# The start of a pooling-mixer layer: ScalarE and VectorE in source order through the first two products

## The chip, the cores and the metric

The kernel runs on one core of a Trainium2 chip. The core has TensorE (matmuls, into eight PSUM banks), VectorE, ScalarE and GpSimd (elementwise work), and SyncE, which here only issues DMAs; DMAs are also issued from ScalarE's and GpSimd's queues. An engine executes its own instructions in the order in which they stand in the program, and waits on semaphores for what others make. The time is device microseconds of one execution, of which several are run and the median is given. One execution is also taken by the hardware profiler, and every row of a profile below is from it.

## The reference

One layer over x (1 x 4096 x 1024, float32):

```python
normed = rms_norm(h, norm_w)
u, gate = split(normed @ in_w, 2)              # in_w 1024 x 2048
pooled = trailing means of u (windows 2, 4, 8, 16; one per group of 256 columns) - u
mixed = einsum('bsgc,gcd->bsgd', pooled, group_w) + group_b
h = h + (mixed * scale * silu(gate)) @ out_w   # out_w 1024 x 1024
out = rms_norm(h, final_norm_w)
```

## The kernel before

**Products.** Every large product (gate half, u half, output) is made with a seven-product scheme for 2 x 2 blocks (P1 to P7): 28 products for the gate half ("a", four blocks of 1024 rows), 28 for the u half ("b"), 56 for the output ("o"). Float32 operands are split in a high and a low part, and each product is three matmuls, high by high, high by low, low by high. One product of "a" or "b" is 48 matmul groups of 128x512 on TensorE. The group's linear map commutes with the trailing mean, so it is folded into the columns of in_w once, at the start ("fold", L406, with its evictions L424 and L171).

**The tiles.** `w[P1]`, `w[P2]` ... hold the split weights of a product, two tiles each (one for each half of its depth). `op0` to `op3` (op_85 to op_88 in the order listings) hold split activations, two for a product. Banks 0 to 7 are bank_69 to bank_76 in these listings. `st` and `vt` tiles are general 128x1024 buffers, taken and given back in turn; `early` tiles are room inside weight tiles that no product uses yet. `ru[q, k]` are quarters of in_w to be folded, loaded by `load_wut`.

**Row scales.** Rows of x are loaded (`load_row`), squared and summed on ScalarE (`square_row`), and `stats` makes 1/sqrt: square root on ScalarE, reciprocal on VectorE (L218), then four small operations that sharpen it (the first block's on VectorE, L157 and L224; later blocks' on GpSimd, L230 to L235). For block 0, `split_rs` and `spread_rs` broadcast the scales over the partitions through TensorE (L472) and bank 7. For later blocks the scales are stored to DRAM (L455) and loaded back as a broadcast (L492), both issued by GpSimd. `normalize` multiplies x with them, and `split_halves` makes an operand's high part (copy on ScalarE) and low part (subtraction on VectorE).

**Sums for the later products.** S1 to S4 are differences and sums of blocks of x, T1 to T4 of weights. `form_s4` makes S4, P3's operand; `rest_of_first` makes P5's weights (T1 of the scheme), P4's (T4) and the copies for P3 during the first block.

**What sets the order.** A scheduler orders instructions by priority and by when their inputs are ready. Inside stretches where `in_line[0]` is True, each instruction that `lined()` records is put behind the one made before it on that engine, so that ScalarE and VectorE keep source order. Before the change this stretch ends ahead of the first product; behind it single edges (`tc.issue_after`) and `tc.high_priority()` hold parts of the order. `run(n, between, behind)` writes product n, calls `between[g]` ahead of its g-th group (key 8: behind the last), and `behind` names the group that is put after the broadcast.

**After P1 and P2.** From L1321 on, a loop runs over the remaining products: it loads, forms and splits operands some products ahead, and evicts and pools behind. Block 1 of the gate half follows block 0's P3. Its P1 and P2 add up in banks 0 to 3; P7 comes third and needs these banks emptied.

Of the kernel before, what the change touches and what calls it, by code (L numbers as in the profile page):

```python
# [61 lines left out]
def kernel(  # L62
# [208 lines left out]
    def pair(cs, h, kh):  # L271
        k = 4 * kh + 2 * h
        return cs[k : k + 2]
# [105 lines left out]
    def load_wut(q, k, queues=(nc.sync,)):  # L379
        r = take("p (k t c) -> p k t c", early5, k=2, t=4)  # L380
        by = 2 // len(queues)
        for n, queue in enumerate(queues):
            kk = slice(n * by, (n + 1) * by)
            queue.dma_start(out=r[:, kk], in_=wut[q, k // 2, :, kk])
        return r
# [12 lines left out]
    def fold(g, r, ps2, halves=(0, 1)):  # L398

        pairs = [(r, g)] if not isinstance(r, list) else [(r[0], g[0]), (r[0], g[1]), (r[1], g[0])]  # L400
        for kk in halves:
            for j in range(2):
                for t in range(2):
                    for m, (a, b) in enumerate(pairs):
                        maps = b[:, 2 * j + t, :]
                        latest[0] = nc.tensor.matmul(  # L406
                            ps2[kk][:, j * 256 : (j + 1) * 256],
                            a[:, kk, 2 * j + t, :],
                            maps if len(pairs) == 1 else woven(maps),
                            start=t + m == 0,  # L410
                            stop=t == 1 and m == len(pairs) - 1,
                        ).ins
        if len(pairs) == 1 and 1 in halves:
            give(r)
# [593 lines left out]
    def load(n):  # L1008
        kind, b, i = step(n)
        if kind == "o":  # L1010
            load_o(b, i)
        elif kind:
            load_in(kind == "b", b, i)
# [82 lines left out]
    for j in range(2, 4):  # L1096
        load_row(0, 0, j)
# [6 lines left out]
    ru[1, 4] = load_wut(1, 4)  # L1104
# [6 lines left out]
    v1[0] = take()  # L1111
# [24 lines left out]
    square_row(0, 0, 3)  # L1136
    for j in range(4):
        load_row(0, 1, j, early if j < 3 else None)
    load(1)
# [7 lines left out]
    fold(gw[1], ru[1, 4], pairs_of[1], (0,))  # L1147
    wut_high(1, 2, w[P2][0])
    spread_rs(0)
    fold(gw[1], ru[1, 4], pairs_of[1], (1,))  # L1150
# [3 lines left out]
    for kk in range(2):  # L1154
        evict_fold(o[1], 4, kk, pairs_of[1], False)
    form(0)
    split_step(0)
    first_split = latest_split[0]
    split_scaled(w[P1][0], g0[0], pair(norm_c, 0, 0))
# [9 lines left out]
    in_line[0] = False  # L1169
    stores.extend((wvd[n], o[j]) for j, n in enumerate((0, 2, 1, 3)))  # L1170

    def second_side(h):

        if h == 1:
            with tc.issue_after(first_split):
                sub(v0[h], v1[h], v0[h])
        with tc.issue_after(first_split):
            for j, c in enumerate(pair(norm_c, h, 0)):
                nc.vector.scalar_tensor_tensor(
                    out=g0[h][:, j], in0=g0[h][:, j], scalar=c, in1=v0[h][:, j],  # L1180
                    op0=ALU.mult, op1=ALU.add,
                )

    second_side(0)
    give(gw[1])
    second_side(1)
    for j in range(4):
        square_row(0, 1, j)
    form(1)
    with tc.high_priority():  # L1190
        rs = stats(0, 1)
    with tc.issue_after(roots[1][0]):
        split_step(1)
    second_split = latest_split[1]
    with tc.issue_after(roots[1][0]), tc.issue_after(roots[1][1]):
        split_scaled(w[P2][0], g1[0], pair(norm_c, 0, 1))

    def copy_first(c):
        def go():
            with tc.issue_after(second_split):  # L1200
                copied.append(copy(banks[4 + c], banks[c]))
        return go

    def copy_and_spread():
        copy_first(1)()
        with tc.high_priority():
            split_rs(1, rs)
        with tc.high_priority():
            spread_rs(1)

    run(0, {6: copy_first(0), 7: copy_and_spread}, 7)
    with tc.issue_after(latest_split[0]), tc.issue_after(latest_split[1]):
        split_scaled(w[P2][1], g1[1], pair(norm_c, 1, 1))
    s = xs[0]
    s["2"] = [take(pool=early) for _ in range(2)]
    split_up[2] = []
    for h in range(2):
        with tc.issue_after(latest_split[0]) if h else nullcontext():
            for key in ("21", "22"):
                normalize(0, 1, s[key][h])  # L1220
        sub(s["21"][h], s["11"][h], s["21"][h])
        added = sub(s["2"][h], s["22"][h], s["21"][h]).ins
        with tc.issue_after(added), tc.issue_after(latest_split[1]):
            split(w[P6][h], g0[h])
        with tc.high_priority():
            split_up[2] += split_halves([s["2"][h]])
    give(rstd.pop(0))
    run(1)
# [65 lines left out]
    for n in range(2, len(steps)):  # L1294
# [28 lines left out]
        if normal:  # L1323
            with tc.issue_after(latest_split[0]):
                form(n + 2)
        if n == 2:
# [11 lines left out]
        if n == 2:  # L1338
            with tc.issue_after(latest_split[0]):
                form_s4(0)  # L1340
            for u in xs[0].pop("2"):
                give(u)
# [83 lines left out]
```

## Time and profile before

| | us |
|---|---|
| median of 3 runs (lowest to highest) | 922.37 (921.27 to 922.46) |
| the profiled execution's own time | 922.1 |
| its span | 920.3 |
| TensorE busy | 904.3 (98%) |
| VectorE busy | 710.0 (77%) |
| ScalarE busy | 458.8 (50%) |
| GpSimd busy | 51.6 (6%) |

The span runs from the first to the last instruction of the profile; the own time holds what lies around it too. The shares are means over stages of different kinds. What matters for a change at the start is when each engine's wait ends there, and which engine it waits for. A row of a timeline gives the start, the time, engine, line, operation, output and input by their names, shape and count, and in brackets the idle time ahead of it with what ended it.

### The profile page before, as it was taken

How to read it: one execution, taken by the hardware profiler on the slowest of the kernel's cores; microseconds unless marked ns; L12 is line 12 of the kernel's file. 1: busy time of each engine (PE TensorE's matmuls, PEld its weight loads, DVE VectorE, ACT ScalarE, POOL GpSimd, SP SyncE). 2: the span in 40 equal slices, each digit the busy share in tenths (PEclk: the TensorE clock that was granted, in tenths of full speed). 3: DMA queues.
4: the chain of work that ended last, by engine and by line, in shares of the span. 5: the costliest groups of instructions: out<-in, count | busy, mean ns of one | idle time of the engine just before them, and what ended most of it. 6: DMA issues, size and time to landing. Idle time of an engine off the chain costs nothing.

```text
span 920.3 us, 11261 instructions
## 1 busy us (share of the span) xinstructions
PE 904.3 (98%) x4230; PEld 789.6 (86%) x4230; DVE 710.0 (77%) x776; ACT 458.8 (50%) x740; POOL 51.6 (6%) x130
## 2 busy tenths in 40 slices
PE   9999989999999999999999999999999999999996
PEld 7888768888888888888888888888888888888886
DVE  5899893886798997496697589589988678677675
ACT  6869437447545565345445545654524424324333
POOL 0024101001100000000000000000001001001010
PEclk9999999999999999999999999999999999999999
DMA  9985774657758636116704626646656446356122
GB/s 350 408 344 171 253 269 136 209 197 275 251 199 273 214 115 207 45 47 215 265 32 140 240 114 206 237 154 203 226 183 233 145 152 229 118 203 209 44 92 92
DMA packets 62550, 177.02 MB, mean 192 GB/s; under 512 B 6048, under 2 KB 22816, under 8 KB 62496
## 3 DMA queue, kind: packets, MB, share of 16 engines
q1 hardware_dynamic: 55920, 154.78, 48.3%
q10 hardware_dynamic: 4176, 13.65, 3.8%
q0 software_dynamic: 2400, 7.88, 2.5%
q8 instruction: 33, 0.54, 0.2%
q14 instruction: 21, 0.17, 0.1%
HBM read 115.45 MB, written 60.83 MB: 192 GB/s over the span
## 4 chain that ended last, share of the span: by engine, by line
PE 86%; DVE 6%; ACT 3%; DMA 3%; issue 2%; SPq 0%; ACTq 0%; DVEq 0%; POOLq 0%
PE bank L621 84%; DVE st L157 2%; DVE vt L157 1%; ACT early L171 1%; DVE op L157 1%; DMA st<-in_x 1%; PE bank L406 1%; DMA st<-rd 1%; ACT w L171 1%; DMA rd<-rs 0%; PE bank L1066 0%; ACT op L171 0%; DMA st<-in_xt 0%; DVE st L732 0%; DVE w L157 0%
## 5 line engine op out<-in xcount | busy, mean ns | idle before, releaser
L621 PE MATMUL bank<-op,w 128*128 128x512 f32 x2688 | 583.2, 380 | 5.8 <-ACT st L171 4.3
L621 PEld LDWEIGHTS bank<-op,w 128*128 128x128 f32 x2688 | 508.9, 189 | 79.4 <-ACT st L171 4.7
L621 PE MATMUL bank<-w,op 128*128 128x512 f32 (+1 forms) x1356 | 290.3, 377 | 0.0
L621 PEld LDWEIGHTS bank<-w,op 128*128 128x128 f32 x1356 | 254.6, 189 | 35.8
L157 DVE TENSOR_TENSOR op<-st,op 128x1024 fp32r<-128x1024 f32 x117 | 142.5, 1220 | 66.6 <-ACT op L171 66.6
L171 ACT ACTIVATE op<-st 128x1024 fp32r<-128x1024 f32 x117 | 123.1, 1054 | 137.2 <-PE bank L621 124.5
L171 ACT ACTIVATE op<-vt 128x1024 fp32r<-128x1024 f32 x49 | 51.5, 1053 | 86.2 <-PE bank L621 65.0
L157 DVE TENSOR_TENSOR st<-st,st 128x1024 f32<-128x1024 f32 (+1 forms) x62 | 73.5, 1203 | 12.2 <-DMA st<-sd 4.4
L157 DVE TENSOR_TENSOR op<-vt,op 128x1024 fp32r<-128x1024 f32 x49 | 59.5, 1221 | 19.5 <-ACT op L171 19.4
L171 ACT ACTIVATE vt<-bank 128x512 f32<-128x512 f32 x94 | 53.4, 592 | 38.9 <-PE bank L621 37.1
L964 DVE TENSOR_TENSOR st<-bank,st 128x512 f32<-128x512 f32 x60 | 41.1, 687 | 31.1 <-PE bank L621 30.9
L171 ACT ACTIVATE bank<-bank 128x512 f32<-128x512 f32 x48 | 27.6, 580 | 31.5 <-PE bank L621 31.5
L214 POOL TENSOR_SCALAR oms<-oss 128x2 f32<-128x2 f32 x14 | 9.2, 656 | 602.0 <-ACT st L853 595.9
L157 DVE TENSOR_TENSOR w<-st,w 128x1024 fp32r<-128x1024 f32 x22 | 26.7, 1219 | 15.2 <-ACT w L171 15.2
L171 ACT ACTIVATE st<-bank 128x512 f32<-128x512 f32 x36 | 20.7, 597 | 28.7 <-PE bank L621 16.4
L157 DVE TENSOR_TENSOR vt<-bank,vt 128x512 f32<-128x512 f32 (+1 forms) x51 | 33.3, 677 | 1.9 <-PE bank L621 1.9
L702 DVE TENSOR_TENSOR_SCAN vt<-vt,bf 128x512 f32<-128x512 f32 x28 | 34.5, 1269 | 0.2 <-ACT vt L171 0.2
L964 DVE TENSOR_TENSOR vt<-bank,vt 128x512 f32<-128x512 f32 (+1 forms) x37 | 24.8, 673 | 12.0 <-PE bank L621 11.7
L171 ACT ACTIVATE w<-st 128x1024 fp32r<-128x1024 f32 x22 | 23.0, 1054 | 18.5 <-PE bank L621 15.0
L171 ACT ACTIVATE vt<-vt 128x1024 f32<-128x1024 f32 (+1 forms) x18 | 18.1, 1011 | 24.0 <-DVE vt L157 16.8
L724 DVE SCALAR_TENSOR_TENSOR vt<-vt,vt 128x1024 f32<-128x1024 f32 x24 | 29.1, 1213 | 0.0
L157 DVE TENSOR_TENSOR vt<-vt,vt 128x1024 f32<-128x1024 f32 x23 | 27.8, 1216 | 1.5 <-DMA vt<-rd 1.3
(116 smaller groups left out, 529.0 us busy)
## 6 DMA issues: line engine op xcount, KB each, us to landing
st<-in_x SPq DMA_DIRECT2D x36, 512.0 KB, 5.2
st<-sd SPq DMA_DIRECT2D x28, 512.0 KB, 4.6
st<-in_xt SPq DMA_DIRECT2D x23, 512.0 KB, 5.8
vt<-in_x SPq DMA_DIRECT2D x21, 512.0 KB, 4.8
st<-yd SPq DMA_DIRECT2D x19, 512.0 KB, 4.3
sd<-st ACTq DMA_DIRECT2D x18, 512.0 KB, 3.3
yd<-st SPq DMA_DIRECT2D x17, 512.0 KB, 2.7
out<-st SPq DMA_DIRECT2D x17, 512.0 KB, 3.8
```

Source lines behind the costliest of these rows:

```text
L157: made.append(nc.vector.tensor_tensor(out=dst, in0=a, in1=b, op=op))
L171: made.append(nc.scalar.activation(dst, src, func, **how))
L214: nc.gpsimd.tensor_scalar(out=ms, in0=ss, scalar1=1.0 / D, scalar2=EPS, op0=ALU.mult, op1=ALU.add)
L406: latest[0] = nc.tensor.matmul(ps2[kk][:, j * 256 : (j + 1) * 256], a[:, kk, 2 * j + t, :], maps if len(pairs) == 1 else woven(maps), star ...
L621: latest[0] = nc.tensor.matmul(ps, a, b, start=start and n == 0, stop=stop and n == 2, skip_group_check=True).ins
L702: nc.vector.tensor_tensor_scan(s[:, j, at:end], v[:, j, at:end], v[:, j, at - win : end - win], sums_of[j] if sums_of else 0.0, ALU.add, A ...
L724: nc.vector.scalar_tensor_tensor(out=s[:, :, at : at + H], in0=s[:, :, at : at + H], scalar=1.0 / win, in1=v[:, :, HIST:], op0=ALU.mult, o ...
L964: partial["added"] = nc.vector.tensor_tensor(out=dst, in0=src, in1=dst, op=ALU.add).ins
```

## The change

The stretch in source order goes on through the first two products. Ahead of and between them the code is rewritten in the order that the engines are to keep. In particular:

- Row 3 of half 0 is loaded between the two 256 KB pieces of quarter (1, 4)'s weights, which were one 512 KB DMA.
- The loads for P2's activations (`load(1)`) go ahead of half 1's rows on SyncE's queue.
- The first `spread_rs` stands one group of fold matmuls later; P2's first normalize and split stand ahead of half 1's statistics; the second `spread_rs` stands behind P1 (and P2 behind it) instead of ahead of P1's last group.
- The weights of P2's second half, S2's parts and `w[P6]` are made in a fixed order.
- `form_s4(0)` moves from step 2 to step 3 of the loop.

```diff
@@ -376,12 +376,14 @@
             )
         return g
 
-    def load_wut(q, k, queues=(nc.sync,)):
+    def load_wut(q, k, queues=(nc.sync,), between=None):
         r = take("p (k t c) -> p k t c", early5, k=2, t=4)
         by = 2 // len(queues)
         for n, queue in enumerate(queues):
             kk = slice(n * by, (n + 1) * by)
             queue.dma_start(out=r[:, kk], in_=wut[q, k // 2, :, kk])
+            if between and n == 0:
+                between()
         return r
 
     def high_part(place, u, pattern, **sizes):
@@ -395,11 +397,11 @@
 
         return [flat[:, j].rearrange(pattern, **sizes) for j in range(2)], low_part
 
-    def fold(g, r, ps2, halves=(0, 1)):
+    def fold(g, r, ps2, halves=(0, 1), sides=(0, 1)):
 
         pairs = [(r, g)] if not isinstance(r, list) else [(r[0], g[0]), (r[0], g[1]), (r[1], g[0])]
         for kk in halves:
-            for j in range(2):
+            for j in sides:
                 for t in range(2):
                     for m, (a, b) in enumerate(pairs):
                         maps = b[:, 2 * j + t, :]
@@ -410,7 +412,7 @@
                             start=t + m == 0,
                             stop=t == 1 and m == len(pairs) - 1,
                         ).ins
-        if len(pairs) == 1 and 1 in halves:
+        if len(pairs) == 1 and 1 in halves and 1 in sides:
             give(r)
 
     def evict_fold(o, k, kk, ps2, is_woven, vector=False):
@@ -1093,22 +1095,21 @@
     raw_ident = take(pool=early)
     nc.sync.dma_start(out=raw_ident[:, 0, 0:P], in_=eye)
     ident = w[P7][1][:, 0, 0, 0:P]
-    for j in range(2, 4):
-        load_row(0, 0, j)
+    load_row(0, 0, 2)
     gw0, gw0_low = high_part(w[P6][0], gw[0], "p (t c) -> p t c", t=4)
     gw0_low()
     v0[0] = take(pool=early)
     evict_fold(v0[0], 0, 0, pairs_of[0], False)
     fold(gw[0], ru[0, 4], pairs_of[1])
     give(gw[0])
-    ru[1, 4] = load_wut(1, 4)
+    ru[1, 4] = load_wut(1, 4, (nc.sync, nc.sync), lambda: load_row(0, 0, 3))
+    v1[0] = take()
     wut_high(0, 2, w[P2][0])
     wut_low(0, 2)
     evict_fold(v0[0], 0, 1, pairs_of[0], False)
     ru[1, 2] = load_wut(1, 2)
     load(0)
     wut_high(0, 6, w[P2][1])
-    v1[0] = take()
     evict_fold(v1[0], 4, 0, pairs_of[1], False, True)
     wut_low(0, 6)
     ru[1, 6] = load_wut(1, 6)
@@ -1134,9 +1135,9 @@
     for kk in range(2):
         evict_fold(v1[1], 6, kk, pairs_of[3], True, True)
     square_row(0, 0, 3)
+    load(1)
     for j in range(4):
         load_row(0, 1, j, early if j < 3 else None)
-    load(1)
     g1 = [load_rows(gate_w, 4 + 2 * h, 0) for h in range(2)]
     load(2)
     fold(gw1, wut_parts[1, 0], pairs_of[0])
@@ -1145,17 +1146,18 @@
     rs = stats(0, 0)
     split_rs(0, rs)
     fold(gw[1], ru[1, 4], pairs_of[1], (0,))
+    fold(gw[1], ru[1, 4], pairs_of[1], (1,), (0,))
     wut_high(1, 2, w[P2][0])
     spread_rs(0)
-    fold(gw[1], ru[1, 4], pairs_of[1], (1,))
+    fold(gw[1], ru[1, 4], pairs_of[1], (1,), (1,))
     evict_fold(o[0], 0, 1, pairs_of[0], True, True)
     wut_low(1, 2)
     o.append(take(pool=early5))
-    for kk in range(2):
-        evict_fold(o[1], 4, kk, pairs_of[1], False)
+    evict_fold(o[1], 4, 0, pairs_of[1], False)
     form(0)
     split_step(0)
     first_split = latest_split[0]
+    evict_fold(o[1], 4, 1, pairs_of[1], False)
     split_scaled(w[P1][0], g0[0], pair(norm_c, 0, 0))
     fold(gw1, wut_parts[1, 2], pairs_of[2])
     o.append(take(pool=early5))
@@ -1166,66 +1168,71 @@
     o.append(take(pool=early5))
     for kk in range(2):
         evict_fold(o[3], 6, kk, pairs_of[3], False)
+    stores.extend((wvd[n], o[j]) for j, n in enumerate((0, 2, 1, 3)))
+    give(gw[1])
+
+    def second_side(h):
+
+        for j, c in enumerate(pair(norm_c, h, 0)):
+            with lined("vector") as made:
+                made.append(
+                    nc.vector.scalar_tensor_tensor(
+                        out=g0[h][:, j], in0=g0[h][:, j], scalar=c, in1=v0[h][:, j],
+                        op0=ALU.mult, op1=ALU.add,
+                    )
+                )
+
+    def bank_copy(c):
+        copied.append(copy(banks[4 + c], banks[c]))
+
+    second_side(0)
+    s = xs[0]
+    for u in s["12"]:
+        normalize(0, 0, u)
+    for j in range(2):
+        square_row(0, 1, j)
+    up = split_halves(s["12"][:1])
+    stores.extend(zip(sd[0][P2], s["12"]))
+    for j in range(2, 4):
+        square_row(0, 1, j)
+    sub(v0[1], v1[1], v0[1])
+    rs = stats(0, 1)
+    last, u = next_op("p (s a b) -> p s a b", s=2, a=2), s["12"][1]
+    copy(last[:, 0], u)
+    split_rs(1, rs)
+    sub(last[:, 1], u, last[:, 0].bitcast(F32))
+    split_up[1] = up + [last]
+    split_scaled(w[P2][0], g1[0], pair(norm_c, 0, 1))
+    second_side(1)
+
+    def copy_and_spread():
+        in_line[0] = True
+        for c in range(2):
+            bank_copy(c)
+        spread_rs(1)
+        for c in range(2, 4):
+            bank_copy(c)
+        in_line[0] = False
+
     in_line[0] = False
-    stores.extend((wvd[n], o[j]) for j, n in enumerate((0, 2, 1, 3)))
-
-    def second_side(h):
-
-        if h == 1:
-            with tc.issue_after(first_split):
-                sub(v0[h], v1[h], v0[h])
-        with tc.issue_after(first_split):
-            for j, c in enumerate(pair(norm_c, h, 0)):
-                nc.vector.scalar_tensor_tensor(
-                    out=g0[h][:, j], in0=g0[h][:, j], scalar=c, in1=v0[h][:, j],
-                    op0=ALU.mult, op1=ALU.add,
-                )
-
-    second_side(0)
-    give(gw[1])
-    second_side(1)
-    for j in range(4):
-        square_row(0, 1, j)
-    form(1)
-    with tc.high_priority():
-        rs = stats(0, 1)
-    with tc.issue_after(roots[1][0]):
-        split_step(1)
-    second_split = latest_split[1]
-    with tc.issue_after(roots[1][0]), tc.issue_after(roots[1][1]):
-        split_scaled(w[P2][0], g1[0], pair(norm_c, 0, 1))
-
-    def copy_first(c):
-        def go():
-            with tc.issue_after(second_split):
-                copied.append(copy(banks[4 + c], banks[c]))
-        return go
-
-    def copy_and_spread():
-        copy_first(1)()
-        with tc.high_priority():
-            split_rs(1, rs)
-        with tc.high_priority():
-            spread_rs(1)
-
-    run(0, {6: copy_first(0), 7: copy_and_spread}, 7)
-    with tc.issue_after(latest_split[0]), tc.issue_after(latest_split[1]):
-        split_scaled(w[P2][1], g1[1], pair(norm_c, 1, 1))
-    s = xs[0]
+    run(0, {8: copy_and_spread})
+    in_line[0] = True
+    normalize(0, 1, s["21"][0])
+    split_scaled(w[P2][1], g1[1], pair(norm_c, 1, 1))
+    normalize(0, 1, s["22"][0])
     s["2"] = [take(pool=early) for _ in range(2)]
     split_up[2] = []
     for h in range(2):
-        with tc.issue_after(latest_split[0]) if h else nullcontext():
+        if h:
             for key in ("21", "22"):
                 normalize(0, 1, s[key][h])
         sub(s["21"][h], s["11"][h], s["21"][h])
-        added = sub(s["2"][h], s["22"][h], s["21"][h]).ins
-        with tc.issue_after(added), tc.issue_after(latest_split[1]):
-            split(w[P6][h], g0[h])
-        with tc.high_priority():
-            split_up[2] += split_halves([s["2"][h]])
+        sub(s["2"][h], s["22"][h], s["21"][h])
+        split(w[P6][h], g0[h])
+        split_up[2] += split_halves([s["2"][h]])
+    in_line[0] = False
     give(rstd.pop(0))
-    run(1)
+    run(1, None, 0)
     with tc.issue_after(latest_split[1]):
         for h in range(2):
             copy(w[P7][h][:, 0], v0[h])
@@ -1323,6 +1330,11 @@
         if normal:
             with tc.issue_after(latest_split[0]):
                 form(n + 2)
+        if n == 3:
+            with tc.issue_after(latest_split[0]):
+                form_s4(0)
+            for u in xs[0].pop("2"):
+                give(u)
         if n == 2:
             with tc.issue_after(first_saves[0]):
                 for place, u in stores:
@@ -1335,11 +1347,6 @@
         if kind == "a" and b == 0:
             with tc.issue_after(latest_split[0]):
                 rest_of_first(n)
-        if n == 2:
-            with tc.issue_after(latest_split[0]):
-                form_s4(0)
-            for u in xs[0].pop("2"):
-                give(u)
         if kind == "a" and b == 2 and i == P4:
             store_t3()
         pool_due(n)
```

Three places of the engines' orders. First ScalarE, from the end of block 0's P6 (banks 4 to 7, evicted to vt_105 or vt_106 and st_89) to the square root of block 1's first half (tmp_0_695, tmp_0_694 after). `early` rows with ss are block 1's row squares; w_0 and w_1 are weights of P5; op_85 and op_86 are its operands. Before:

```order
L171 ACTIVATE op_85<-st_93 128x1024
L171 ACTIVATE st_89<-bank_75 128x512
L171 ACTIVATE st_89<-bank_76 128x512
L171 ACTIVATE w_0_627<-early_1_109 128x1024
L171 ACTIVATE early_0_108,ss_0_689<-early_0_108 128x1024
L171 ACTIVATE w_1_628<-early_0_110 128x1024
L171 ACTIVATE early_0_110,ss_0_689<-early_0_110 128x1024
L171 ACTIVATE early_1_111,ss_0_689<-early_1_111 128x1024 x2
L171 ACTIVATE op_86<-st_94 128x1024
L171 ACT_TABLE_LOAD
L171 ACTIVATE tmp_0_695<-ss_0_689,eps 128x4
```

In the changed kernel the same stretch of ScalarE reads:

```order
L171 ACTIVATE st_89<-bank_75 128x512
L171 ACTIVATE st_89<-bank_76 128x512
L171 ACTIVATE early_0_108,ss_0_688<-early_0_108 128x1024
L171 ACTIVATE early_0_110,ss_0_688<-early_0_110 128x1024
L171 ACTIVATE early_1_111,ss_0_688<-early_1_111 128x1024
L171 ACTIVATE w_0_628<-early_1_109 128x1024
L171 ACTIVATE w_1_629<-early_0_110 128x1024
L171 ACTIVATE early_1_111,ss_0_688<-early_1_111 128x1024
L171 ACTIVATE op_85<-st_94 128x1024
L171 ACT_TABLE_LOAD
L171 ACTIVATE tmp_0_694<-ss_0_688,eps 128x4
L171 ACTIVATE op_86<-st_95 128x1024
```

The squares and the square root now stand ahead of op_86's copy, and three squares ahead of the weight copies and op_85's.

Second VectorE, in the same stretch: w_0 and w_1 are P5's low parts, vt_100 and vt_101 (st_99 and vt_100 after) are S4, the operations on vt_102 and vt_103 with colt T4, and L218 is the reciprocal for block 1. Before:

```order
L157 TENSOR_TENSOR op_85<-st_93,op_85 128x1024
L157 TENSOR_TENSOR w_0_627<-early_1_109,w_0_627 128x1024
L157 TENSOR_TENSOR w_1_628<-early_0_110,w_1_628 128x1024
L157 TENSOR_TENSOR vt_100<-vt_100,early_0_108 128x1024
L157 TENSOR_TENSOR vt_101<-vt_101,early_1_109 128x1024
L157 TENSOR_TENSOR op_86<-st_94,op_86 128x1024
L1255 SCALAR_TENSOR_TENSOR vt_102<-vt_102,colt,st_96 128x512
L218 RECIPROCAL rs_0_696<-tmp_0_695 128x4
L1255 SCALAR_TENSOR_TENSOR vt_102<-vt_102,colt,st_96 128x512
L1255 SCALAR_TENSOR_TENSOR vt_103<-vt_103,colt,st_97 128x512 x2
```

In the changed kernel the same stretch of VectorE reads:

```order
L157 TENSOR_TENSOR w_0_628<-early_1_109,w_0_628 128x1024
L157 TENSOR_TENSOR w_1_629<-early_0_110,w_1_629 128x1024
L157 TENSOR_TENSOR op_85<-st_94,op_85 128x1024
L218 RECIPROCAL rs_0_695<-tmp_0_694 128x4
L157 TENSOR_TENSOR op_86<-st_95,op_86 128x1024
L157 TENSOR_TENSOR st_99<-st_99,early_0_108 128x1024
L157 TENSOR_TENSOR vt_100<-vt_100,early_1_109 128x1024
L1262 SCALAR_TENSOR_TENSOR vt_102<-vt_102,colt,st_96 128x512 x2
L1262 SCALAR_TENSOR_TENSOR vt_103<-vt_103,colt,st_97 128x512 x2
```

The reciprocal now stands ahead of op_86's low part, S4 and T4; S4 stands behind both of P5's operands.

Third ScalarE around the evictions of block 1's first two products (banks 0 to 3, bank_69 to bank_72), ahead of its P7. st_92 holds a pooled result until its store is done; sd rows are stores of operands, and vt_104 with ss is a row's square. Before:

```order
L171 ACTIVATE op_88<-st_98 128x1024
L516 DMA sd_4_0_151<-st_97 128x1024
L516 DMA sd_4_1_152<-vt_101 128x1024
L171 ACTIVATE st_92<-bank_69 128x512
L171 ACTIVATE st_92<-bank_70 128x512
L171 ACTIVATE st_96<-bank_71 128x512
L171 ACTIVATE st_96<-bank_72 128x512
L171 ACTIVATE vt_104,ss_0_1143<-vt_104 128x1024
```

In the changed kernel ScalarE has there:

```order
L171 ACTIVATE op_88<-st_98 128x1024
L518 DMA sd_7_1_150<-st_98 128x1024
L518 DMA sd_4_0_151<-st_97 128x1024
L171 ACTIVATE st_96<-bank_71 128x512
L171 ACTIVATE st_96<-bank_72 128x512
L171 ACTIVATE vt_104,ss_0_1144<-vt_104 128x1024
L171 ACTIVATE st_92<-bank_69 128x512
L171 ACTIVATE st_92<-bank_70 128x512
```

The evictions into st_96 and one square now stand ahead of those into st_92.

## The prediction

> **What bounds the kernel now.** I read the page's totals first, then what TensorE waits for, then the chain of work that ended last, and then the timelines of VectorE, ScalarE and GpSimd over the first 136 us, since the change touches nothing later.
>
> ```profile
> span 920.3 us, 11261 instructions
> PE 904.3 (98%) x4230; PEld 789.6 (86%) x4230; DVE 710.0 (77%) x776; ACT 458.8 (50%) x740; POOL 51.6 (6%) x130
> ```
>
> TensorE is busy for 904.3 of 920.3 us. No product goes away here (the few new rows on TensorE are groups cut in two by the order), so the change can only act on the 16 us of idle time, and on the clock. Where the idle time lies:
>
> ```profile
> PE bank L621 <- ACT st L171: 4.3, 1, 4.3
> PE bank L621 <- DVE op L157: 1.4, 2, 0.9
> PE bank L472 <- DVE hl L157: 0.9, 1, 0.9
> PE bank L472 <- ACT hl L171: 0.8, 1, 0.8
> PE bank L406 <- DVE tmp L224: 0.7, 1, 0.7
> ```
>
> Columns: total us, times, longest. The 4.3 us is one wait. The timeline of TensorE places it:
>
> ```profile
> 110.47 19.48 PE L621 MATMUL bank<-op,w 128*128 128x512 f32 x89 [0.90 <-DVE op L157]
> 134.29 6.05 PE L621 MATMUL bank<-op,w 128*128 128x512 f32 x19 [4.34 <-ACT st L171]
> ```
>
> TensorE finishes block 1's second product at 129.95 and starts the third (P7) only at 134.29. From there the windows show it full:
>
> ```profile
> 135.00:136.00 1.00, 1.00 (x4) 0.50 0.83 229
> 138.00:139.00 1.00, 1.00 (x6) 0.91 0.63 258
> 140.00:200.00 60.00, 60.00 (x280) 1.00 0.56 186
> ```
>
> (Columns: busy time, TensorE's own with its count, granted clock, DMA share, GB/s.) After the wait the clock is at half from about 134.6 to 138.0, which costs some 1.7 us of work; later all runs at 1.00. So 134.29 is a gate: all that TensorE wins or loses before it (the 0.7, 0.8, 0.9 and 1.4 above) only lengthens or shortens the wait there. What the change is worth is how far the gate moves. The chain says what the gate hangs on:
>
> ```profile
> 77.21 0.17 DVE rs L218
> 84.62 4.60 DMA rd<-rs
> 89.62 6.25 DMA st<-rd
> ...
> 128.56 1.34 DVE st L732 x2
> 129.92 3.64 DMA yd<-st
> 133.64 0.61 ACT st L171
> 134.29 15.77 PE bank L621 x64
> ```
>
> Read from below: P7 needs bank 0 emptied; ScalarE empties it into st_92; st_92 still holds a pooled result that must be stored first; VectorE makes that result (L732) at the end of a list with one small gap since 95.89 (its row is below), where it had waited 3.30 for block 1's row scales (row sums, square root, reciprocal at 77.21, GpSimd's four small operations, store, broadcast load). Two inputs meet at 95.89: VectorE's own list, and those scales. I follow both.
>
> **The change, part by part.** The rows of VectorE and their neighbours that give the prices:
>
> ```profile
> 22.53 1.20 PE L472 MATMUL bank<-w,hl 128*128 128x128 f32 x8
> 24.42 2.35 DVE L157 TENSOR_TENSOR st<-st,st 128x1024 f32<-128x1024 f32 x2
> 27.21 2.36 DVE L157 TENSOR_TENSOR op<-st,op 128x1024 fp32r<-128x1024 f32 x2 [0.44 <-ACT op L171]
> 37.38 0.18 DVE L218 RECIPROCAL rs<-tmp 128x4 f32<-128x4 f32 x1 [1.25 <-ACT tmp L171]
> 44.80 0.75 DVE L248 SCALAR_TENSOR_TENSOR w<-vt,colt,w 128x512 fp32r<-128x512 f32 x1 [0.79 <-ACT w L171]
> 47.27 1.22 DVE L157 TENSOR_TENSOR st<-st,st 128x1024 f32<-128x1024 f32 x1
> 75.40 1.23 DVE L157 TENSOR_TENSOR op<-st,op 128x1024 fp32r<-128x1024 f32 x1 [0.39 <-ACT op L171]
> 77.29 2.05 DVE L1255 SCALAR_TENSOR_TENSOR vt<-vt,colt,st 128x512 f32<-128x512 f32 x3
> 85.79 2.36 DVE L157 TENSOR_TENSOR w<-st,w 128x1024 fp32r<-128x1024 f32 x2 [1.30 <-ACT w L171]
> 90.16 0.18 DVE L218 RECIPROCAL rs<-tmp 128x4 f32<-128x4 f32 x1 [0.22 <-ACT tmp L171]
> 95.89 2.36 DVE L157 TENSOR_TENSOR st<-st,st 128x1024 f32<-128x1024 f32 x2 [3.30 <-DMA st<-rd]
> 114.66 1.23 DVE L157 TENSOR_TENSOR op<-st,op 128x1024 fp32r<-128x1024 f32 x1 [0.69 <-ACT op L171]
> ```
>
> From the x2 row at 24.42 and the single one at 47.27, a full-width operation costs 2.35 − 1.22 = 1.13 in a series; from 77.29, a half-width T4 operation 0.665.
>
> *1. Weights in two pieces around row 3.* Half of a 512 KB load now goes ahead of the last row on SyncE's queue.
>
> ```profile
> 12.00:21.00 9.00, 8.26 (x74) 1.00 1.04 413
> 10.61 7.84 DMA st<-in_x
> ```
>
> At 413 GB/s, with the engines full (1.04), 262 KB cost 0.63 us. Row 3 landed at 18.45; its square, the square root and the first scales follow. The broadcast of those scales by TensorE (22.53) waited for TensorE too, and is put three matmuls later in a group of 1.97 us, while TensorE's 0.74 wait ahead of it goes. I take +0.43 for VectorE's first normalize (24.42 to 24.85). Bounds: 0, if the broadcast was bound by TensorE; +1.2, if row 3 is put back by the whole load.
>
> *2. VectorE to 47.27.* The set of operations is the same (half-1 statistics and P2's first normalize change places). Three pauses stood there, 0.44 + 1.25 + 0.79 = 2.48. The 1.25 goes: the square root now has four full operations (4.5 us) in front of it, and that also covers the half-1 rows, which land two 512 KB loads (2.5 us) later. The other two I leave. Against that, six tiny operations of the statistics now stand behind one another and show their 0.2 each, where they hid between big ones at 0.1: +0.6. Sum: +0.43 − 1.25 + 0.6 = −0.2. The halves' broadcast now stands behind P1 on TensorE: 0.8 + 0.9 of waiting go, P2 starts some 2 us sooner, and P6's second operand then stops it for about 1. TensorE reaches the gate near 127, so it stays early.
>
> *3. 47.27 to 69.25.* The same list: −0.2 stays.
>
> *4. ScalarE and the block 1 statistics.* The fourth square, the square root and so the reciprocal come sooner in ScalarE's list, for two evictions and three squares now precede op_85's copy. A full-width activation takes 1.05, and about 1.0 in a series.
>
> ```profile
> 74.32 1.05 ACT L171 ACTIVATE op<-st 128x1024 fp32r<-128x1024 f32 x1
> 75.39 1.28 ACT L171 ACT_TABLE_LOAD   x1
> 76.68 0.30 ACT L171 ACTIVATE tmp<-ss,eps 128x4 f32<-128x4 f32 x1
> ```
>
> P6 ends at about 64.6 (64.4 plus an eviction's start). From there: two evictions 1.1, three squares with the reading of their sums 3.1, two weight copies 1.9, the fourth square 1.0, op_85 1.0, table load 1.3, root 0.2: 74.3, before 76.9. The reciprocal comes at 74.5 instead of 77.21, that is 2.7 sooner. The price is VectorE's: it is ready for the first weight at 69.05 and now waits for ScalarE at four places, 0.8 (weight copy done 69.85), 0.65 (op_85, 72.75), 0.5 (the root), 0.8 (op_86, 75.35) = 2.7, where it had 0.39. S4 and T4 end at 79.26 − 0.2 + 2.7 − 0.39 = 81.4.
>
> *5. GpSimd's part.* Its four operations stood partly behind VectorE:
>
> ```profile
> 77.53 0.55 POOL L230 TENSOR_TENSOR tmp<-rs,ms 128x4 f32<-128x4 f32 x1 [2.46 <-DVE rs L218]
> 78.82 5.11 POOL L232 TENSOR_SCALAR tmp<-tmp 128x4 f32<-128x4 f32 x1
> 84.02 0.20 POOL L235 TENSOR_TENSOR rs<-rs,tmp 128x4 f32<-128x4 f32 x1
> ```
>
> The L232 operation took 5.11 us on a 128x4 tile; VectorE ran two-input operations on SBUF without a break from 79.26 to 83.80. While VectorE ran T4 (77.29 to 79.26), which also reads a column of scalars, the same engine needed 0.55. [...] In the new order the reciprocal falls into VectorE's pause for op_86, then come op_86's low part and S4 (three full operations, 3.4 us), then T4. So the four operations end by T4's window, 79.9 at the latest. Plus 0.4, the store 4.60, 0.4, the load 6.25: the scales land by 91.6. Before, 95.87.
>
> *6. VectorE to block 1's first normalize.* From 79.26 to 95.89 lay 1.30 + 0.22 + 3.30 = 4.82 of pauses, so 11.8 of work; the same set follows now. The 3.30 goes (scales at 91.6). A pause of about 1 comes: the last row of block 1's other half is loaded into the tile of the T4 weights, after T4, so its square and the second reciprocal (90.16 before) come at 91.
>
> ```profile
> 82.78 0.33 SPq L437 DMA_DIRECT2D vt<-in_x  x1
> ```
>
> (Issue at 82.78 before, 84.9 by step 4; then its landing, square and root as before.) 81.4 + 11.8 + 1.0 = 94.2: 1.7 sooner than 95.89. Bounds: 93.2 without that pause, 95.9 if both steps 4 and 6 cost a microsecond more.
>
> *7. From there to the gate.* The same operations lead to the pooled result in st_92, less the 0.69 pause at 114.66 (op copies come sooner on ScalarE): the end of L732, 129.9 in the chain, becomes 129.9 − 1.7 − 0.7 = 127.5. The store (3.64, and 0.1 around it) ends at 131.2. ScalarE has a new order there: two evictions into st_96 and a square stand ahead of st_92's. st_96 is free two full operations behind the result, 129.7; two evictions 1.1 and the square 1.05 give 131.8. TensorE resumes 0.65 behind: about 132.3, before 134.29. That is 2.0 us.
>
> *8. The clock.* TensorE's wait grows from 4.3 to over 5 us, and I keep the same 1.7 us at half clock; bounds 0 and +1.7. [...]
>
> S4 and T4 moved by a step cost nothing by themselves: their readers are products P4 and P3, tens of microseconds later. The DMA cut in two adds one issue on SyncE.
>
> **The sum.** The profiled execution took 922.1 us of its own (span 920.3). 922.1 − 2.0 = 920.1; it lies 0.3 under the median of the runs, 922.37, so the median should come to 920.4.
>
> **The rivals.**
> *B, more of it passes.* If the four waits of step 4 do not come (ScalarE runs ahead, or VectorE's list is later by other means), VectorE is at 81.4 − 2.3 and the normalize waits for the scales, 91.6 or a little sooner; then the gate moves by another 2 to 3 us, as far as the ScalarE order at the end (square, evictions) allows: 917.6. For it speaks that ScalarE is only half busy; against it that the list in step 4 has no gap to give.
> *C, the gate stays.* Late row 3 at its bound (+0.8 more) and the second reciprocal 1 us later than I say leave nothing of the 1.7: 922.4. For it speaks that each of the pauses removed was short and the next thing was due soon after.
> *D, slower: GpSimd starved.* If its last operation does not end in T4's window, about 81.4, VectorE's next stretch has six two-input operations (6.8 us, to 88.2), as it had in 79.26 to 83.80. It then ends behind the bank additions, about 89, and the scales land at 89 + 0.4 + 4.6 + 0.4 + 6.25 = 100.6; the normalize is 4.7 later than 95.89, the gate by 4 at least: 926.5. The point that decides is 84.2, where the last operation ended before. For it speaks the 5.11 row; against it the pauses of VectorE just then (step 4). [...]
>
> **How the numbers follow.** The forecast has 0.50 (its own range 919.0 to 921.8, from the bounds of steps 1, 6 and 8), B 0.20, C 0.14, D 0.16. A change of under 0.2% (1.8 us: 920.5 to 924.2) is about what a measurement of this kernel cannot tell from none. The forecast lies on that edge: 0.30 of its 0.50 counts as faster, 0.20 as same. Faster 0.30 + 0.20 = 0.50; same 0.20 + 0.14 = 0.34; slower 0.16. The range leaves out D and a little of B: 917.5 to 922.9.
>
> **What would show it.** Steps 1 and 2: the first normalize near 24.9, VectorE at 47.1. Step 4: the reciprocal near 74.5, waits of VectorE for ScalarE of some 2.7 us between 69 and 77. Step 5: GpSimd's last small operation before 80. Step 6: no wait for the row scales at block 1's normalize, near 94.2. Step 7: P7 of block 1 near 132.3 after a wait of about 5 us. It is wrong if the normalize still waits for scales, if ScalarE's end of the list holds the eviction, or if TensorE waits before 127 by so much that it comes to the gate late.

## The result, and the profile after

| | before | after |
|---|---|---|
| median of 5 runs each (us) | 921.27 (920.31 to 922.46) | 917.0 (915.27 to 918.13) |
| ratio, 95% interval | | 0.9948 (0.9931 to 0.9966) |
| span of the profiled execution | 920.3 | 916.4 |
| block 1's P7 starts | 134.29 | 130.49 |
| TensorE idle ahead of it | 4.34 | 3.82 |

The kernel is 0.5% faster, 4.3 us by the medians and 3.9 us by the two spans. The forecast was 920.4 with a range of 917.5 to 922.9. It had the right direction, but its gain of 2.0 us is half of what the spans show and less than half by the medians, and 917.0 lies below its range. The start of P7 moved by 3.80 us, so nearly all of the 3.9 lies ahead of that gate. The page of the changed kernel, and what TensorE waits for:

```profile
span 916.4 us, 11265 instructions
PE 904.3 (99%) x4230; PEld 789.3 (86%) x4230; DVE 710.3 (78%) x776; ACT 459.2 (50%) x740; POOL 48.2 (5%) x130
```

```profile
PE bank L623 <- ACT st L171: 3.8, 1, 3.8
PE bank L1068 <- PEq L1418: 0.8, 1, 0.8
PE bank L623 <- ACT op L171: 0.4, 1, 0.4
```

The small waits ahead of the gate are gone, 0.74, 0.81 and 0.91 us at the front and 0.54 and 0.90 at 108 to 110; one of 0.44 is new. TensorE's busy time is the same 904.3. Idle time for data was 8.2 us before and is 4.3 now, and that difference is the 3.9 us of the spans. The half-rate stretch behind the gate cost about the same in these two executions, 3.4 us at 0.50 in each, some 1.7 us of work (an estimate, half of that time). In the changed kernel:

```profile
130.00:132.00 2.00, 1.51 (x6) 0.86 1.00 406
132.00:134.00 2.00, 2.00 (x6) 0.50 0.65 150
134.00:136.00 2.00, 2.00 (x9) 0.79 0.92 352
136.00:138.00 2.00, 2.00 (x11) 1.00 0.84 311
```

(Windows of the changed kernel: busy time, TensorE's own with its count, granted clock, DMA share, GB/s.) VectorE's timeline answers to the rows shown of before:

```profile
24.71 2.36 DVE L157 TENSOR_TENSOR st<-st,st 128x1024 f32<-128x1024 f32 x2 [0.46 <-ACT st L171]
46.60 1.22 DVE L157 TENSOR_TENSOR st<-st,st 128x1024 f32<-128x1024 f32 x1
69.39 2.36 DVE L157 TENSOR_TENSOR w<-early,w 128x1024 fp32r<-128x1024 f32 x2 [0.72 <-ACT w L171]
72.32 1.23 DVE L157 TENSOR_TENSOR op<-st,op 128x1024 fp32r<-128x1024 f32 x1 [0.57 <-ACT op L171]
73.93 0.18 DVE L218 RECIPROCAL rs<-tmp 128x4 f32<-128x4 f32 x1 [0.39 <-ACT tmp L171]
74.88 1.23 DVE L157 TENSOR_TENSOR op<-st,op 128x1024 fp32r<-128x1024 f32 x1 [0.77 <-ACT op L171]
78.29 2.74 DVE L1262 SCALAR_TENSOR_TENSOR vt<-vt,colt,st 128x512 f32<-128x512 f32 x4
92.89 0.18 DVE L218 RECIPROCAL rs<-tmp 128x4 f32<-128x4 f32 x1 [2.66 <-ACT tmp L171]
95.23 2.35 DVE L157 TENSOR_TENSOR st<-st,st 128x1024 f32<-128x1024 f32 x2
```

Block 1's first normalize comes at 95.23, where it came at 95.89: of all that moved on VectorE only 0.66 us is left there. The pooled result that goes into st_92 (L734 now) ended at 129.9 before and ends at 128.2: 1.65 us sooner. The gate moved by 3.80. So 2.15 us were won behind VectorE's list, on the last link, and the chain that ended last shows it:

```profile
126.92 1.32 DVE st L734 x2
128.25 1.14 DVE st L157
...
129.41 0.33 ACTq L518
...
129.84 0.60 ACT st L171
...
130.49 19.65 PE bank L623 x82
```

Before, the chain had a store of 3.64 us (DMA yd<-st) in this place. Now it has one normalize (1.14), the issue of a DMA by ScalarE, and an eviction. The order of TensorE's instructions tells why. At the start of block 1's P7 stood, before,

```
L621 MATMUL bank_69<-op_87,w_0_83 128x512 x6
L621 MATMUL bank_70<-op_87,w_0_83 128x512 x6
L621 MATMUL bank_71<-op_87,w_0_83 128x512 x6
L621 MATMUL bank_72<-op_87,w_0_83 128x512 x6
L621 MATMUL bank_69<-op_88,w_1_84 128x512 x6
```

and in the changed kernel

```
L623 MATMUL bank_71<-op_87,w_0_83 128x512 x6
L623 MATMUL bank_72<-op_87,w_0_83 128x512 x3
L623 MATMUL bank_69<-op_87,w_0_83 128x512 x6
L623 MATMUL bank_70<-op_87,w_0_83 128x512 x6
L623 MATMUL bank_72<-op_87,w_0_83 128x512 x3
```

P7 now starts on banks 2 and 3 (bank_71, bank_72). ScalarE empties these first, into st_96, the tile of block 1's row scales. It is free as soon as the normalizes that read it are done, and no store stands in between. Banks 0 and 1 are emptied into st_92 later, while P7 already runs. No line of the diff says this: the scheduler chose it.

### The profile page after: what moved, and what is told of

Its sections match the earlier page's. It is cut to its first block, busy times and chain, and to the rows that moved or that the text cites. A ratio compares the mean times of both kernels' runs of the same rounds, so it can differ in the third digit from the quotient of the medians.

```text
span 916.4 us, 11265 instructions
## 1 busy us (share of the span) xinstructions
PE 904.3 (99%) x4230; PEld 789.3 (86%) x4230; DVE 710.3 (78%) x776; ACT 459.2 (50%) x740; POOL 48.2 (5%) x130
## 4 chain that ended last, share of the span: by engine, by line
PE 88%; DVE 6%; ACT 3%; issue 1%; DMA 1%; ACTq 0%; DVEq 0%
PE bank L623 85%; PE bank L408 2%; DVE st L157 2%; DVE vt L157 1%; DVE op L157 1%; ACT early L171 1%; DMA vt<-in_x 1%; ACT w L171 1%; DVE w L157 1%; PE bank L1068 0%; DVE vt L1262 0%; DVE vt L734 0%; DVE st L734 0%; DVE vt L726 0%; ACT vt L171 0%
## 5 line engine op out<-in xcount | busy, mean ns | idle before, releaser
L157 DVE TENSOR_TENSOR op<-st,op 128x1024 fp32r<-128x1024 f32 x121 | 147.6, 1222 | 76.7 <-ACT op L171 76.7
L171 ACT ACTIVATE op<-st 128x1024 fp32r<-128x1024 f32 x121 | 127.1, 1052 | 147.0 <-PE bank L623 129.1
L171 ACT ACTIVATE op<-vt 128x1024 fp32r<-128x1024 f32 x45 | 47.2, 1053 | 82.1 <-PE bank L623 67.3
L157 DVE TENSOR_TENSOR st<-st,st 128x1024 f32<-128x1024 f32 (+1 forms) x64 | 76.0, 1205 | 8.0 <-ACT st L256 3.2
L157 DVE TENSOR_TENSOR op<-vt,op 128x1024 fp32r<-128x1024 f32 x45 | 54.8, 1223 | 8.4 <-ACT op L171 8.3
L171 ACT ACTIVATE vt<-vt 128x1024 f32<-128x1024 f32 (+1 forms) x22 | 22.3, 1014 | 19.1 <-DVE vt L157 15.4
L157 DVE TENSOR_TENSOR vt<-vt 128x1024 f32<-128x1024 f32 (+1 forms) x24 | 28.7, 1222 | 0.0
```

What stands on the lines that cost most here:

```text
L157: made.append(nc.vector.tensor_tensor(out=dst, in0=a, in1=b, op=op))
L171: made.append(nc.scalar.activation(dst, src, func, **how))
```

## The experiments

Each time is a median beside runs of the kernel before on the same chip; "before" was 921.28 beside the first four and 921.42 beside the last four.

### The last link undone, and done alone

In the changed kernel, ScalarE is held to the order 0, 1, 2, 3 for these four evictions:

```diff
             ev["11"] = [take() for _ in range(2)]
+            in_line[0] = b == 1 and q == 0
             for c, u in enumerate(cells(ev["11"])):
                 last = copy(halved(u), plain(ps[c]), AF.Silu)
+            in_line[0] = False
```

> The changed kernel, but ScalarE empties the four banks of block 1's first two products in the order 0, 1, 2, 3 (as before the change), and TensorE's P7 starts on bank 0 again; nothing of VectorE's order changes. Theory 'last link': of the 3.8 us by which the gate moved, some 2.1 come from P7 starting on bank 2, whose eviction goes into a tile that a normalize sets free, and not a store. Then P7 resumes near 132.6 (end of the pooled result 128.16, store issued 128.27, 3.64 us, eviction 0.65) and not at 130.49, and the kernel takes about 919.1. Rival 'list': VectorE's earlier list is the whole gain, and the store would be done in time anyway: P7 resumes by 130.9, 917.0 to 917.4.

Measured: 920.75, ratio to before 0.9996 (0.9981 to 1.0011). Without the link nothing of the gain can be told from noise. TensorE and the evictions, by the timelines of this kernel:

```profile
131.80 18.52 PE L623 MATMUL bank<-op,w 128*128 128x512 f32 x71 [5.35 <-ACT st L171]
```

```profile
131.15 2.06 ACT L171 ACTIVATE st<-bank 128x512 f32<-128x512 f32 x4 [11.57 <-DMA yd<-st]
```

The wait for the store (yd<-st) is back. The pooled result ended at 127.2 in this execution, and P7 started 4.6 us behind that; in the changed kernel the distance is 2.3, before it was 4.5. So the link is worth some 2.2 us, as expected. The time is 1.6 us worse than expected, and the clock gives a reason: the half-rate stretch was longer in this execution, 0.50 still at 134 to 136 and 0.56 at 136 to 138:

```profile
132.00:134.00 2.00, 2.00 (x5) 0.50 0.86 272
134.00:136.00 2.00, 2.00 (x6) 0.50 0.26 104
136.00:138.00 2.00, 2.00 (x7) 0.56 0.61 199
138.00:140.00 2.00, 2.00 (x11) 1.00 0.16 64
```

The other runs agree with it. The mean granted clock of each run is on record: 0.993 to 0.995 in nine of the ten runs of this kernel, 0.996 to 0.998 in the five of the changed kernel. A thousandth of the clock is some 0.9 us of 920 (an estimate). So the 3.75 us between the two medians are not the link's alone; whether the longer wait brought the lower clock with it is not shown. What the link is worth is read at the gate.

The other way round, the kernel before with banks 2 and 3 emptied first:

```diff
+            in_line[0] = b == 1 and q == 0
+            parts = list(enumerate(cells(ev["11"])))
-            for c, u in enumerate(cells(ev["11"])):
+            for c, u in parts[2:] + parts[:2] if in_line[0] else parts:
                 last = copy(halved(u), plain(ps[c]), AF.Silu)
+            in_line[0] = False
```

> The kernel before, with the evictions of block 1's first two products in the order 2, 3, 0, 1 alone; TensorE's P7 then starts with bank 2. Theory 'last link': the gate goes from 134.29 to about 133.2 (the second normalize on that tile ends at 132.2, and two stores issued by ScalarE stand ahead of the eviction), so the kernel is about 1.1 us faster than before. Rival 'list': no difference, within 0.3 us.

Measured: P7 at 132.87 instead of 134.29, with a wait of 3.32; 920.82, ratio 0.9994 (0.9984 to 1.0005).

```profile
132.87 17.45 PE L621 MATMUL bank<-op,w 128*128 128x512 f32 x72 [3.32 <-ACT st L171]
```

The gate moved as the theory said (133.2 expected). The pooled result ended 0.4 us sooner in this execution, so the link gave 1.0 of the 1.4. In the time it does not show beyond the interval. The link's gain is half of what the changed kernel has, because here ScalarE issues two stores ahead of the eviction, the second of which waits for a second normalize; in the changed kernel one of them stands behind.

### The second half's statistics behind the normalize

VectorE waited 2.66 us at 92.89 for a square root whose result is needed only some 18 us later, and the normalize of block 1's first half stood behind it. Here that reciprocal is put behind the normalize:

```diff
-                if j % 4 == 3:
+                if j % 4 == 3 and (n, j) != (5, 7):
                     scales[j // 4] = stats(b + 1, j // 4)
...
         if normal:
             with tc.issue_after(latest_split[0]):
                 form(n + 2)
+        if n == 5:
+            with tc.issue_after(normalized[0]):
+                scales[1] = stats(1, 1)
```

> The changed kernel, with the statistics of block 1's second half (the reciprocal on VectorE for which it waited 2.66 us at 92.89) behind the normalize of the first half. Theory: this wait took back most of what the new order had won on VectorE; without it the normalize comes at 92.6 instead of 95.23, P7 of block 1 resumes near 128, and the time falls by 2.6 to 4 us (the last 1.5 if the shorter wait leaves the clock at full rate): 913 to 914.4. Rival: the second half's scales, which start later, then come too late for their normalize near 111.5, and the wait comes back there: 916.3 or more.

Measured: 913.24 (913.17 to 913.62), ratio to before 0.9912 (0.9893 to 0.9932). It has the lowest median of this study. VectorE and TensorE:

```profile
92.86 2.35 DVE L157 TENSOR_TENSOR st<-st,st 128x1024 f32<-128x1024 f32 x2
95.13 0.17 DVE L218 RECIPROCAL rs<-tmp 128x4 f32<-128x4 f32 x1
```

```profile
129.17 21.00 PE L625 MATMUL bank<-op,w 128*128 128x512 f32 x96 [0.59 <-ACT st L171]
```

```profile
130.00:132.00 2.00, 2.00 (x11) 1.00 0.71 141
132.00:134.00 2.00, 2.00 (x11) 1.00 0.98 365
```

The normalize is 2.4 us sooner, and the clock stays at full rate. The wait of 0.59 us is not ahead of P7 but inside it. TensorE's row before it shows that, and so does an eviction by ScalarE:

```profile
58.82 69.76 PE L625 MATMUL bank<-op,w 128*128 128x512 f32 x319 [0.44 <-ACT op L171]
```

```profile
125.81 0.60 ACT L171 ACTIVATE st<-bank 128x512 f32<-128x512 f32 x1 [7.33 <-PE bank L625]
```

The first row holds 319 matmuls, where the changed kernel has 312 up to the start of P7. So seven of P7's ran without a wait, from 126.9 on, on a bank that ScalarE emptied at 125.81, as soon as TensorE was done with it. The scheduler gave the last link another order here too. The span fell by 4.6 us against the changed kernel's. Of this 3.2 is idle time of TensorE (4.26 to 1.03); the other 1.4 is about what half rate had cost (some 1.7). How much of it is the earlier normalize and how much the new order at the end, this run does not tell apart. The rival's late scales did not come: the second half's normalizes show no wait for them.

### S4 in step 2 again

```diff
+        if n == 2:
+            with tc.issue_after(latest_split[0]):
+                form_s4(0)
+            for u in xs[0].pop("2"):
+                give(u)
...
-        if n == 3:
-            with tc.issue_after(latest_split[0]):
-                form_s4(0)
-            for u in xs[0].pop("2"):
-                give(u)
```

> The changed kernel with S4 formed in step 2 again. Theory: S4's place is worth nothing at the gate, since the normalize at 95.23 waited for the second half's reciprocal and not for the row scales, which land at about 87: 917.0, at most 0.5 us either way. Rival: S4's place is what brought the first reciprocal forward, and with S4 ahead of it again the scales gate the normalize: 918.5.

Measured: 914.28 (913.76 to 914.95), ratio to before 0.9923 (0.9903 to 0.9943). Neither of the two had it: with S4 in step 2 the changed kernel is some 2.5 us faster (2.3 by the two ratios, 2.7 by the medians, which are of two chips). VectorE's timeline shows how:

```profile
71.50 1.22 DVE L157 TENSOR_TENSOR st<-st,early 128x1024 f32<-128x1024 f32 x1
72.63 1.22 DVE L157 TENSOR_TENSOR vt<-vt,early 128x1024 f32<-128x1024 f32 x1
73.77 0.17 DVE L218 RECIPROCAL rs<-tmp 128x4 f32<-128x4 f32 x1
73.85 2.33 DVE L157 TENSOR_TENSOR op<-st,op 128x1024 fp32r<-128x1024 f32 x2
76.10 2.73 DVE L1262 SCALAR_TENSOR_TENSOR vt<-vt,colt,st 128x512 f32<-128x512 f32 x4
```

The two S4 operations (71.50 and 72.63) stand where the changed kernel waits for ScalarE (0.57, 0.39 and 0.77). They need nothing of ScalarE, and the reciprocal is as early as with them behind. T4 starts at 76.10, not 78.29. The tile of block 1's last row comes free so much sooner, and the normalize is at 92.33. TensorE waits 0.54 us at P7 and the clock stays at full rate (1.00 over 124 to 140). ScalarE's end of the list is another here as well: one eviction at 126.84, and the other three behind a store at 129.10. So the 2.5 us are those of S4's place together with what the scheduler made of it.

### Both edits together

> The changed kernel with both edits that had helped: S4 formed in step 2 again, and the second half's statistics behind block 1's first normalize. Theory: each alone brought the gate to where TensorE itself arrives (127 to 128.5, with waits of 0.5 us left), so both together win little more: 912.8 to 914.3, with no wait of TensorE at block 1's P7. Rival: the two gains are of separate waits and add up: 910 to 911.5.

Measured: 914.23 (913.72 to 914.57), ratio 0.9912 (0.9896 to 0.9929). The gains do not add. The reciprocal's wait has gone, but another of 1.82 us stands in its place ahead of the normalize:

```profile
91.19 1.23 DVE L157 TENSOR_TENSOR op<-vt,op 128x1024 fp32r<-128x1024 f32 x1 [1.82 <-ACT op L171]
92.33 2.35 DVE L157 TENSOR_TENSOR st<-st,st 128x1024 f32<-128x1024 f32 x2
```

ScalarE's copy for this operand stands behind the square of that last row in its own list. TensorE has waits of 0.44, 0.47, 0.41 and 0.20 us left.

### The second broadcast in P1 again

```diff
         for c in range(2):
             bank_copy(c)
         spread_rs(1)
-        for c in range(2, 4):
-            bank_copy(c)
         in_line[0] = False
...
-    run(0, {8: copy_and_spread})
+    run(0, {7: copy_and_spread}, 7)
...
-    run(1, None, 0)
+    run(1)
```

> The changed kernel with the second broadcast of row scales ahead of P1's last group again, as before the change, with TensorE's waits around it. Theory: TensorE loses 1 to 2 us at 41 to 44 again, but all of this is taken from its wait at block 1's P7, and the time is that of VectorE's list, whose order this edit also moves (S4 ahead of the reciprocal again, the fourth square behind the weight copies): between 914 and 917.5. Rival: TensorE's waits at the front count, and the kernel is 1 to 2 us slower than the changed one: 918 to 919.

Measured: 915.26 (914.62 to 915.65), ratio 0.9923 (0.9906 to 0.994). The time is as the theory had it, but for a half-wrong reason: TensorE does not wait at the broadcast at all.

```profile
40.73 1.20 PE L474 MATMUL bank<-w,hl 128*128 128x128 f32 x8
41.76 17.54 PE L623 MATMUL bank<-op,w 128*128 128x512 f32 x79
```

So the waits of 0.81 and 0.91 of before were not those of the place. The changed kernel beside it on the same chip took 917.67 (ratio 0.9944, 0.9923 to 0.9966). The edit moves VectorE's and ScalarE's lists at 65 to 80 as well, so that S4's first operation stands ahead of the reciprocal; T4 ends at 80.4, where it ended at 81.8 in the changed kernel's execution beside it. What of the 2.4 us is the broadcast's place and what that order's, this run does not tell apart.

### Row 3 ahead of the whole quarter

```diff
-    load_row(0, 0, 2)
+    for j in range(2, 4):
+        load_row(0, 0, j)
...
-    ru[1, 4] = load_wut(1, 4, (nc.sync, nc.sync), lambda: load_row(0, 0, 3))
+    ru[1, 4] = load_wut(1, 4)
```

> The changed kernel with row 3 loaded ahead of the whole 512 KB quarter again. Theory: row 3 lands 0.6 us sooner, TensorE waits up to 0.7 us at 21 again, VectorE's first normalize moves by less than 0.4 us, and the gate by as much: 916.6 to 917.4. Rival: the fold's weights in front were the gain at the start: slower by 0.7 us or more.

Measured: 918.42 (917.63 to 919.7), ratio to before 0.9964 (0.9944 to 0.9983), beside 917.67 (916.07 to 919.19) of the changed kernel:

> The changed kernel as it is, beside the next three on one chip: 917.0, P7 of block 1 resumes near 130.5 after a wait of 3.8 us.

The 0.75 between them has the size that the rival named (0.7 or more), but it lies within both ranges. TensorE waited 0.96 at 21.15 again, and P7 started at 129.86 here and at 130.34 in the changed kernel's execution. What the two pieces are worth stays open, for the two intervals overlap.

## Why the prediction fell short

**What held.** The gate at P7 was the right place: the waits of TensorE ahead of it vanished, 3.9 us in all (0.44 came new), and its arrival moved from 129.95 to 126.67 (near 127 in the prediction), without the start of P7 being set by that. Step 1: the first normalize at 24.71 (24.85 forecast). Step 2: 46.60 instead of 47.07; the pauses and the tiny operations cost a little less. Step 4: VectorE's four waits were 0.72, 0.57, 0.39 and 0.77, 2.45 us (2.7 forecast), the reciprocal came at 73.93 (74.5), T4 ended at 80.94 (81.4). Step 5: the row scales gated nothing; GpSimd's last small operation ended at 76.16, as S4 began, so rival D had no place.

```profile
75.10 1.06 POOL L235 TENSOR_TENSOR rs<-rs,tmp 128x4 f32<-128x4 f32 x1
```

**Step 7 failed.** It took ScalarE's new order (banks 2 and 3 first) only as two more instructions ahead of st_92's eviction, and let TensorE wait for that eviction. TensorE's own order had followed: P7 starts on bank 2. So the path over the store, 3.64 us and what lies around it, was no longer the path of the gate. The term was taken as a loss of 0.6 us against the end of the store, and was a gain of 2.15 against before. The run with this order undone shows it (P7 4.6 us behind the pooled result instead of 2.3), and so does the one with the order done alone (the link 1.0 us shorter). Of the orders at this place the prediction had ScalarE's and not TensorE's.

**Step 6 was mis-sized.** The pause for the second half's reciprocal was put at 1 us and was 2.66. The tile's reload was issued at 84.46, near the 84.9 that the step took, but it landed 6.84 us later, where the same load had taken 5.0 before:

```profile
84.46 6.84 DMA vt<-in_x
```

Five other 512 KB loads were issued right behind it, four before. The changed kernel's second execution had a pause of 1.66 there, so this term moves by a microsecond between executions. With steps 6 and 7 as measured, VectorE's list gave 1.65 us (2.4 forecast) and the link 2.15: 3.8 instead of 2.0. Two of the prediction's sums are off by a little: the list of step 4 adds up to 74.2 and not 74.3, and 131.8 and 0.65 in step 7 to 132.45 and not 132.3. Neither decides anything.

**Step 8** kept the loss at half rate at 1.7 us for a wait of over 5 us; that it would not grow was the author's estimate. The runs showed some 1.7 us behind the wait of 3.82 here and some 2.9 behind one of 3.11 in the second execution (half of the 3.4 and 5.9 us at 0.50); with bank 0 first, the wait was 5.35 us and the half-rate stretch 6.8 us long.

**S4's move was costed at nothing, and cost some 2.5 us.** The step named the wrong cover. It asked who reads S4, and these readers are indeed late. It did not ask what VectorE would do in S4's old place, though the waits of step 4 are there: S4 was the work that hid them.

**Rival B** had the time (917.6), but not the cause: the four waits came.

## What to carry to other kernels

Where one engine empties several buffers and another refills them, read the orders of both: the wait ends with the buffer that the refilling engine asks for first, and a scheduler may swap it unasked. An operation that can run at any time is worth most in the place where its engine would wait; before moving it, look at what stands still in the gap it leaves. And a result that is needed late should not stand, with a wait of its own, ahead of one that is needed now.

## What the runs showed of the hardware

At the gate TensorE's longer waits had a price beyond their length. The granted clock fell to half around every wait of 2.69 us (row 3 ahead of the whole quarter) to 5.35 us (bank 0 first); with waits of 1.53 us (in the kernel with the second broadcast in P1) and 0.6 or less it stayed at 1.00. Once it also fell behind two shorter waits close together: in the kernel before with banks 2 and 3 first, two waits of 0.88 and 0.91 us end at 41.34 and 42.58, with one small matmul between them, and the clock was at half from 44.1 on:

```profile
44.00:46.00 2.00, 2.00 (x7) 0.52 1.04 410
```

In the kernel before, the same two waits (0.81 and 0.91) left it at 1.00. How long it stayed at half was not given by the wait's length either. The changed kernel had it for 3.4 us in one execution, with a wait of 3.82, and in the other for 6.8 us, the last 5.9 of them behind a wait of 3.11:

```profile
130.00:132.00 2.00, 1.66 (x4) 0.50 0.95 387
132.00:134.00 2.00, 2.00 (x6) 0.50 0.68 137
134.00:136.00 2.00, 2.00 (x6) 0.50 0.97 371
136.00:138.00 2.00, 2.00 (x10) 0.94 0.77 283
```

(The changed kernel's second execution, windows as above.) That is 1.7 or 2.9 us of lost work: the second execution had its P7 a little sooner than the first, but its span was 917.4 instead of 916.4.

What decides it is not shown. In the profiled executions of the kernel before and of the changed kernel, the trace's record of the clock has 3.41 us at half rate at the gate, and 129.71 and 126.29 us at full rate ahead of it, 38 and 37 times as much. Six executions have a fall at the gate. By their windows, half rate lasted about 3.4 us in four of them and 6.8 in two. In these two, the one above and that with bank 0 first, 0.9 us of the wait reached into the stretch at half; in the other four at most 0.05 us did. No run here moves a wait in time and changes nothing else, so this rests on these six alone.

The kernels without the half-rate stretch also repeat better: the runs of the late-reciprocal, S4 and broadcast kernels lie within 0.5, 1.2 and 1.0 us, those of the changed kernel within 3.1 on the chip of the last four experiments and those of before within 5.4. The mean granted clock of each run goes the same way: it was 0.997 to 0.999 in the late-reciprocal, S4 and broadcast kernels. Of the first five runs of the changed kernel, the two at 0.998 took 915.27 and 915.48 us and the three at 0.996 took 917.0 to 918.13. So part of the spread, and of the differences between medians, goes with the clock.

GpSimd's small operations took other times beside VectorE than the 5.11 row of before had led to expect. In the changed kernel the first three of block 1's first half, at 74.26 to 75.01, with VectorE waiting up to 74.88, took 0.19 to 0.20 us each. The four of the second half, from 93.22 on, beside VectorE's two-input operations (1.13 us each in a series), took 1.02 to 1.06 us each:

```profile
93.22 1.02 POOL L230 TENSOR_TENSOR tmp<-rs,ms 128x4 f32<-128x4 f32 x1 [0.41 <-DVE rs L218]
94.31 1.06 POOL L231 TENSOR_TENSOR tmp<-tmp,rs 128x4 f32<-128x4 f32 x1
95.46 1.04 POOL L232 TENSOR_SCALAR tmp<-tmp 128x4 f32<-128x4 f32 x1
```

Here each took about as long as one operation of VectorE; before, the one of 5.11 us ran beside four of them (79.26 to 83.88). What decides between the two was not tried.
